# A decoder layer on one core: norm sums and rows placed apart, first MLP-down operands in freed buffers, residual loaded in gated halves

## The chip, the core and the metric

The kernel runs on one core of a Trainium2 chip. TensorE (PE) multiplies and has a queue of its own for weight loads (PEld); VectorE (DVE), ScalarE (ACT) and GpSimd (POOL) do the elementwise work; SyncE (SP) issues every DMA here, from one queue, in order. Each engine runs its instructions in the order in which the program holds them. The metric is the device time of one execution, in microseconds (us).

## The reference, cut to what matters

```python
u = rms_norm(h, norm_mix_g);  proj = u @ w_in          # attention and mLSTM mixers (left out)
h = h + mix @ w_out                                    # "out projection"
u = rms_norm(h, norm_mlp_g)
h = h + jnp.square(jax.nn.relu(u @ w_up)) @ w_down     # "MLP up", "MLP down"
gate = jax.nn.sigmoid(rms_norm(h, norm_ple_g) @ w_ple_gate)
h = h + gate * (p @ w_ple)                             # "gate"; p @ w_ple are the "pl products"
return rms_norm(h, final_norm_g)
# rms_norm(x, g) = x * rsqrt(mean(x*x) + eps) * g; x is 1024 tokens x 1024 features, w_up 1024 x 4096
```

## The kernel before

Activations lie transposed: 128 features on the partitions, 1024 tokens along a row, so `h` is 8 tiles of 128x1024 fp32. fp32 precision comes from splitting each operand into a high and a low part (`split`: a cast on ACT, L93, then a subtraction on DVE, L94) and multiplying three times (`mm3`: L102 high by high, L103 high by low, L104 low by high). A stage is therefore a chain: raw load by DMA, cast on ACT, subtraction on DVE, three matmuls of 128x512.

A norm has two parts on PE. The squares of all features are added into one tile `state`; its column sums are small matmuls with a vector of ones (`cs`, L125); DVE and POOL turn them into 1/sqrt per token (`ra`, `rb`; the power is L135, L963 or L1030); PE spreads these over all partitions by transposes (`bp`, L131) and ACT copies them out (`rB`). Where the norm stands ahead of a product its weight is folded into the operand and its row factor is multiplied into the product afterwards, so the products themselves need no `rB`.

From the out projection on the stages are, in order of time:

- the norm of MLP up: `rstd_rows` makes column sums and rows in one go;
- the pl products, 96 matmuls, copied out by ACT (L862);
- MLP up, 16 steps f. Each does seven products for a 2x2 block (a Strassen scheme, keys b11, t1, t2, b22, t3, b21, t4), 84 matmuls. POOL makes weight combinations (L753 to L755) and activation combinations (L790); ACT and DVE split both. After each step DVE multiplies by the norm rows (L886), ACT squares (L887), and the results and their four combinations are stored to the DRAM array `zd` in two DMAs (zz, L888; zt, L895);
- MLP down, again seven keys, each over 8 groups g of 24 matmuls. A group loads `y` from `zd` (L977) and weights (L911), and for four of the keys POOL subtracts weights (L925, L928, L932). At the end of a key DVE adds PSUM to `h` (L989). When a half row of `h` is complete (keys b22, t3, b21, t4), `ready` squares it, adds the square to `state` on POOL (L952) and splits it into `hp`;
- the gate: `rstd_half(1)` after t3 and `rstd_half(0)` after t4, products `pg`, and the final norm in three slices of tokens (512, 256, 256).

Each engine's order is made when the program is built: a list scheduler runs its own timeline over the written order and may move an instruction ahead of others. Buffers come from pools; a new tile that lies over an older one waits until the older one's last readers, DMAs included, are done.

Of the kernel before, what the change touches and what calls it, by code (L numbers as in the profile page):

```python
# [16 lines left out]
P = 128  # L17
# [28 lines left out]
def layer_kernel(ctx, tc, xT, wqk, wv, wvg, wmv, wmqk, wmo, wout, wup, wdown, wpg, wple, pT,  # L46
# [667 lines left out]
    with ExitStack() as tail:  # L714
        zp = tail.enter_context(tc.tile_pool(name="zp", bufs=2, reuse_waits="tile"))
        up_scope = ExitStack()
        wtc, zu, wta, wtb = [up_scope.enter_context(tc.tile_pool(name=n, bufs=2, reuse_waits="tile"))
                             for n in ("wtc", "zu", "wta", "wtb")]
        pmm = tail.enter_context(tc.tile_pool(name="pmm2", bufs=8, space=PSUM, reuse_waits="tile"))

        def ztile(name):
            return zu.tile([P, 2, T], F32, name=name, tag="z", bufs=4)

# [92 lines left out]

        def rstd_rows(state, times=None):
            cs = acc_tile("cs2")
            col_sum(cs, state)
            a = zp.tile([P, NB], F32, name="ra", tag="ra")  # L820
            b = zp.tile([P, NB], F32, name="rb", tag="rb")
            rstd_cols(b, cs[:, :NB], a)
            if times is not None:
                G.tensor_tensor(b, b, times, op=ALU.mult)
            dst = zp.tile([P, T], F32, name="rB", tag="rB", bufs=1)
            rows(dst, b)
            return dst

# [23 lines left out]
        wpl = [load_t(wple[k], "wpl") for k in range(2)]  # L852
        rB = rstd_rows(sqs, srec)

# [10 lines left out]


        OWN = (0, 14, 15)
        for f in range(FF // P // 2):
            z = ztile("zz")
# [16 lines left out]
            V.scalar_tensor_tensor(z, z, 0.0, rB.unsqueeze(1).to_broadcast([P, 2, T]), op0=ALU.max, op1=ALU.mult)  # L886
            S.activation(z, z, AF.Square)  # L887
            nc.sync.dma_start(zd[f, :, :4], z.rearrange("p a (c t) -> p (a c) t", t=CH))  # L888
            ts = ztile("zt").rearrange("p a (c t) -> p (a c) t", t=CH)
            c0, c1 = slice(0, CH), slice(CH, T)  # L890
            V.tensor_tensor(ts[:, 0], z[:, 0, c1], z[:, 0, c0], op=ALU.subtract)
            V.tensor_tensor(ts[:, 1], z[:, 1, c1], ts[:, 0], op=ALU.add)
            V.tensor_tensor(ts[:, 2], z[:, 0, c1], z[:, 1, c1], op=ALU.add)
            V.tensor_tensor(ts[:, 3], z[:, 1, c0], ts[:, 1], op=ALU.subtract)
            nc.sync.dma_start(zd[f, :, 4:], ts)  # L895
        up_scope.close()
# [3 lines left out]
        NG = FF // P // 4  # L900
        rawp, hlp = [tail.enter_context(tc.tile_pool(name=n, bufs=3, reuse_waits="tile")) for n in ("rawp", "hlp")]

        def stream(name, tag, bufs):
            return rawp.tile([P, T], F32, name=name, tag=tag, bufs=bufs)

        def parts(name, tag, src):
            return split([hlp.tile([P, T], F32R, name=name + i, tag=tag + i) for i in "hl"], src)

        def wraw(g, blk):
            r = stream("wd_r", "wr", 4)  # L910
            nc.sync.dma_start(r, wdown[g, blk])  # L911
            return r

        A11, A12, A21, A22 = range(4)
        SLOT = dict(b11=0, b21=2, b22=3, t1=4, t2=5, t3=6, t4=7)
        sp4 = [pair("s", F32) for _ in range(NG // 2)]
# [38 lines left out]
        def rstd_half(c):  # L955
            sl = slice(c * CH, (c + 1) * CH)
            n = NB // 2
            cs = acc_tile("cs2")
            col_sum(cs, state[:, sl], n=n)
            a = zp.tile([P, NB], F32, name="ra", tag="ra")  # L960
            b = zp.tile([P, NB], F32, name="rb", tag="rb")
            V.tensor_scalar(a[:, :n], cs[:, :n], 1.0 / D, EPS, op0=ALU.mult, op1=ALU.add)
            G.tensor_tensor(b[:, :n], a[:, :n], mhalf[:, :n], op=ALU.pow)  # L963
            bp = acc_tile("bp2")
            bcast_rows(bp, b, n)
            S.copy(rB[:, sl], bp)

        bank = {}
        for key in OPS:
# [5 lines left out]
            for g in range(NG):  # L975
                y = stream("y_r", "yr", 3)
                nc.sync.dma_start(y.rearrange("p (f t) -> p f t", t=CH),  # L977
                                  zd[2 * g:2 * g + 2, :, SLOT[key]].rearrange("f p t -> p f t"))
                yh, yl = parts("y", "y", y)
                wh, wl = parts("wd", "w", weights(key, g))  # L980
                for o in range(KT // 2):
# [17 lines left out]

        def embed(w, k, sl):  # L1000
            n = sl.stop - sl.start

            def ev(ps, c, sl):
                ga = small("ga")[:, :n]
                V.tensor_tensor(ga, ps, rB[:, sl], op=ALU.mult)
                S.activation(ga, ga, AF.Tanh, scale=0.5)
                V.scalar_tensor_tensor(ga, ga, 1.0, emb[k][:, sl], op0=ALU.add, op1=ALU.mult)
                V.scalar_tensor_tensor(h[k][:, sl], ga, 0.5, h[k][:, sl], op0=ALU.mult, op1=ALU.add)
            proj_chunk(pmm, w, hp, ev, "pg", sl)
            if k == 0:  # L1010
                if not fin:
                    fin.append(unit("fin", F32))
                S.activation(fin[0][:, sl], h[k][:, sl], AF.Square)
            else:
                sq = small("sq3")[:, :n]
                S.activation(sq, h[k][:, sl], AF.Square)
                V.tensor_tensor(fin[0][:, sl], fin[0][:, sl], sq, op=ALU.add)

        def final(i, sl):
            n = sl.stop - sl.start  # L1020
            nt = n // P
            cs = acc_tile("cs3")
            col_sum(cs, fin[0][:, sl], n=nt)
            a = zp.tile([P, nt], F32, name="ra3", tag="ra")
# [3 lines left out]
            else:  # L1028
                V.tensor_scalar(a, cs[:, :nt], 1.0 / D, EPS, op0=ALU.mult, op1=ALU.add)
            G.tensor_tensor(b, a, mhalf[:, :nt], op=ALU.pow)  # L1030
            bp = acc_tile("bp3")
            bcast_rows(bp, b, nt)
            rows = small("rows")[:, :n]
# [28 lines left out]

        for k in range(2):
            fetch(k)
        for c in (1, 0):
            for k in range(2):
                embed(ws[k], k, slice(c * CH, (c + 1) * CH))
        for k in range(2, KT - LATE):
            fetch(k)
            for c in range(NCH):  # L1070
                embed(ws[k], k, slice(c * CH, (c + 1) * CH))
# [89 lines left out]
```

## Time and profile before

| | us |
|---|---|
| median of 3 runs (lowest, highest) | 1453.23 (1449.82, 1454.43) |
| the profiled execution: time | 1451.09 |
| its span in the trace | 1449.3 |
| PE busy | 1350.0 (93%) |
| DVE busy | 987.5 (68%) |
| ACT busy | 621.9 (43%) |
| POOL busy | 415.3 (29%) |

The profile is of one execution. PE is busy for nearly the whole span, so what counts are the places where it stands idle and the places where its granted clock is below full. The two are seen in the table of PE's waits and in rows of its timeline: two matmuls of 128x512 in a row start 0.23 us apart at the full clock and 0.43 us apart at the lower one.

### The profile page before, as it was taken

To read this page: it belongs to the slowest core of one execution; us is meant where nothing else is said; L and a number is where in the kernel's file an instruction comes from. 1 tells how busy PE (TensorE), PEld (TensorE's weight loads), DVE (VectorE), ACT (ScalarE), POOL (GpSimd) and SP (SyncE) were. 2 spreads that over 40 slices of the span, in tenths; PEclk is the share of its full clock that TensorE was granted. 3 is DMA by queue.
4 is the path that set the end of the run, shared out by engine and by line. 5 is a ranking of instruction groups with operands and counts; after the bars stand their busy time and mean duration, and the time that the engine had idled before them with its cause. 6 is when DMAs were issued, how large, how long until landed. Compare 5 with 4: busy or idle time off the path is not lost.

```text
span 1449.3 us, 18272 instructions
## 1 busy us (share of the span) xinstructions
PE 1350.0 (93%) x6815; PEld 1135.3 (78%) x6815; DVE 987.5 (68%) x1462; ACT 621.9 (43%) x975; POOL 415.3 (29%) x261
## 2 busy tenths in 40 slices
PE   8999999999889998949999999995999999898996
PEld 6978988878788886737888888884888888686886
DVE  7788688599767874792476666674589856465455
ACT  6555545644454341344344443442333354343323
POOL 1522120231014220261244333440268423111002
PEclk9999999999999999978999999997999999899998
DMA  6111112123154367423344434447897647464113
GB/s 222 45 48 37 34 47 72 57 84 100 41 169 147 100 228 262 144 104 123 139 156 164 174 146 163 157 174 292 287 310 241 205 131 275 131 198 136 44 44 116
DMA packets 75689, 208.24 MB, mean 144 GB/s; under 512 B 7281, under 2 KB 17425, under 8 KB 70993
## 3 DMA queue, kind: packets, MB, share of 16 engines
q1 hardware_dynamic: 75600, 207.09, 41.5%
q8 instruction: 53, 0.87, 0.3%
q14 instruction: 36, 0.29, 0.1%
HBM read 146.74 MB, written 60.32 MB: 143 GB/s over the span
## 4 chain that ended last, share of the span: by engine, by line
PE 52%; DVE 9%; issue 8%; DMA 4%; POOL 2%; ACT 2%; SPq 0%; DVEq 0%; ACTq 0%; POOLq 0%
PE u L102 7%; PE u L103 7%; PE u L104 7%; PE d L102 7%; PE d L103 7%; PE d L104 7%; DMA in<-mixmd 1%; POOL state L952 1%; PE pl L103 1%; PE pl L102 1%; PE pl L104 1%; PE cs L125 1%; PE mo L102 1%; DMA wo_r<-wout 1%; PE mo L103 1%
## 5 line engine op out<-in xcount | busy, mean ns | idle before, releaser
L102 PE MATMUL d<-yh,wdh 128*128 128x512 f32 x448 | 176.5, 394 | 17.1 <-ACT wdh L93 17.1
L103 PE MATMUL u<-x,wuh 128*128 128x512 f32 x448 | 176.5, 394 | 0.0
L103 PE MATMUL d<-yl,wdh 128*128 128x512 f32 x448 | 176.3, 393 | 0.0
L104 PE MATMUL d<-yh,wdl 128*128 128x512 f32 x448 | 174.4, 391 | 0.0
L102 PE MATMUL u<-x,wuh 128*128 128x512 f32 x448 | 174.3, 395 | 0.0
L104 PE MATMUL u<-x,wul 128*128 128x512 f32 x448 | 171.2, 394 | 0.0
L94 DVE TENSOR_TENSOR wul<-wu_r,wuh 128x768 fp32r<-128x768 f32 (+1 forms) x64 | 71.6, 1119 | 90.0 <-ACT wuh L93 89.8
L102 PEld LDWEIGHTS d<-yh,wdh 128*128 128x128 f32 x448 | 85.2, 190 | 35.4 <-ACT wdh L93 17.6
L753 POOL TENSOR_TENSOR wu_r<-wu_r 128x512 f32<-128x512 f32 x32 | 49.6, 1549 | 211.4 <-DMA wu_r<-wup 176.0
L103 PEld LDWEIGHTS u<-x,wuh 128*128 128x128 f32 x448 | 84.5, 189 | 19.7
L102 PEld LDWEIGHTS u<-x,wuh 128*128 128x128 f32 x448 | 84.4, 188 | 19.7
L104 PEld LDWEIGHTS u<-x,wul 128*128 128x128 f32 x448 | 84.4, 188 | 19.7
L103 PEld LDWEIGHTS d<-yl,wdh 128*128 128x128 f32 x448 | 85.2, 190 | 18.4 <-DVE yl L94 0.6
L104 PEld LDWEIGHTS d<-yh,wdl 128*128 128x128 f32 x448 | 84.9, 189 | 17.7
L94 DVE TENSOR_TENSOR yl<-y_r,yh 128x1024 fp32r<-128x1024 f32 x56 | 92.3, 1648 | 8.0 <-ACT yh L93 7.9
L93 ACT CAST wuh<-wu_r 128x768 fp32r<-128x768 f32 (+1 forms) x64 | 60.4, 943 | 78.9 <-POOL wu_r L754 55.5
L94 DVE TENSOR_TENSOR wdl<-wd_r,wdh 128x1024 fp32r<-128x1024 f32 x32 | 44.8, 1399 | 70.5 <-ACT wdh L93 70.4
L412 ACT ACTIVATE pr<-pr,mn 128x128 f32<-128x128 f32 (+3 forms) x64 | 49.5, 774 | 56.1 <-PE av L415 30.4
L94 DVE TENSOR_TENSOR wdl<-s,wdh 128x1024 fp32r<-128x1024 f32 x24 | 54.1, 2255 | 24.5 <-ACT wdh L93 24.5
L93 ACT CAST wdh<-wd_r 128x1024 fp32r<-128x1024 f32 x32 | 33.6, 1051 | 85.2 <-PE d L103 60.0
L876 ACT COPY tmp<-u 128x512 f32<-128x512 f32 x48 | 28.0, 586 | 85.7 <-PE u L104 85.7
L93 ACT CAST yh<-y_r 128x1024 fp32r<-128x1024 f32 x56 | 58.7, 1048 | 12.3 <-DMA y_r<-zd 10.0
(368 smaller groups left out, 3633.4 us busy)
## 6 DMA issues: line engine op xcount, KB each, us to landing
wd_r<-wdown SPq DMA_DIRECT2D x72, 512.0 KB
y_r<-zd SPq DMA_DIRECT2D x56, 512.0 KB
wu_r<-wup SPq DMA_DIRECT2D x32, 512.0 KB
zd<-zz SPq DMA_DIRECT2D x16, 1024.0 KB
zd<-zt SPq DMA_DIRECT2D x16, 1024.0 KB
wm_r<-wmqk SPq DMA_DIRECT2D x8, 512.0 KB
wo_r<-wout SPq DMA_DIRECT2D x16, 256.0 KB
hs<-h SPq DMA_DIRECT2D x8, 512.0 KB
```

The source lines that it names most:

```text
L93: S.copy(hi, src)
L94: V.tensor_tensor(lo, src, hi.bitcast(F32), op=ALU.subtract)
L102: PE.matmul(ps, wh, xh, start=start, stop=False, skip_group_check=more)
L103: PE.matmul(ps, wh, xl, start=False, stop=False, skip_group_check=more)
L104: PE.matmul(ps, wl, xh, start=False, stop=stop, skip_group_check=more)
L125: PE.matmul(ps[:, off + j:off + j + 1], src[:, j * P:(j + 1) * P], ones, start=start, stop=stop and (start or j == n - 1))
L412: S.activation(pr[:, :nk], pr[:, :nk], AF.Exp, scale=-1.0, bias=mn[:, :1], accum_out=den)
L753: G.tensor_tensor(raw[:, 4:7:2], raw[:, 2:3].to_broadcast([P, 2, L]), raw[:, 1:4:2], op=ALU.subtract)
L876: S.copy(tmp[key], ps)
L952: G.tensor_tensor(state[:, sl], state[:, sl], sq, op=ALU.add)
```

## The change

It has five parts.

1. The norm of MLP up is cut in two. `rstd` (column sums and power) is called after the first step of MLP up, `rows` after the second, and the first step's multiplication, square and stores (`store(0)`) follow it. The pl products come straight after the out projection. The buffers of zz and zt become two pools, zu0 and zu1, taken by even and odd steps.
2. The first two groups' operands of MLP down are loaded into `unit` buffers that MLP up has freed by its last step, and split into `pair` buffers that it frees during that step. The split buffers of the other groups come from two pools: hl2, with two buffers, and hl1, with one, which every third group takes (g3 first) and which lies over zu1.
3. The residual `h`, loaded back in 8 DMAs of 512 KB during the last step of MLP up, is loaded in 16 halves. Ahead of each stands a one-element copy on POOL that reads the group's `yl`; the DMA waits for it.
4. `ready` adds the squares on DVE. `rstd_half(1)` is cut in two and written into key b21; the first three gate products of the second half of tokens, and two of the first half, stand around the other one.
5. At the end, the last tile's squares are not added on DVE but summed on PE by a second row of small matmuls, and a slice's column sums are placed after the first product of the next slice.

The core of the diff:

```diff
-        wtc, zu, wta, wtb = [...]
+        wtc, zu0, wta, wtb, zu1 = [...]
...
-        rB = rstd_rows(sqs, srec)
         for k2 in range(KT // 2):      # pl products
...
+            if f == FF // P // 2 - 2:
+                first = [(y_load(0, unit("y_r", F32), "b11"), w_load(0, unit("wd_r", F32), 0))]
             products([load_blocks(wup[f, i], "wu") for i in range(2)], X, ev, "u", own)
-            (multiply by rB, square, store, four combinations, store)
+            zs.append(z)
+            if f == 0:
+                rcols = rstd(sqs, NB, srec)
+                continue
+            if f == 1:
+                rB = zp.tile([P, T], F32, name="rB", tag="rB", bufs=1)
+                rows(rB, rcols)
+                store(0)
+            store(f)
+        first.append((y_load(1, unit("y_r", F32), "b11"), w_load(1, unit("wd_r", F32), 0)))
+        first = [[split(pair(n), r) for n, r in zip(("y", "wd"), raws)] for raws in first]
         up_scope.close()
-        rawp, hlp = [... bufs=3 each]
+        rawp, hl2, hl1 = [... for n, b in (("rawp", 3), ("hl2", 2), ("hl1", 1))]
         def parts(name, tag, src):
+            pool = hl1 if made[tag] % 3 == 1 else hl2
+            made[tag] += 1
...
         h = [unit("h", F32) for _ in range(KT)]
-        for k in range(KT):
-            nc.sync.dma_start(h[k], hs[k])
+        LOADS = {("b11", 1 + n): (2 * n, lo) for n in range(4)}
+        LOADS.update({("b11" if n < 3 else "t1", (5 + n) % NG): (2 * n + 1, hi) for n in range(4)})
+        LOADS.update({("t2", 1 + n): (2 * n, hi) for n in range(4)})
+        LOADS.update({("b21", 1 + n): (2 * n + 1, lo) for n in range(4)})
...
-                G.tensor_tensor(state[:, sl], state[:, sl], sq, op=ALU.add)
+                V.tensor_tensor(state[:, sl], state[:, sl], sq, op=ALU.add)
...
+                if (key, g) in LOADS:
+                    k, half_of = LOADS[key, g]
+                    G.tensor_copy(h[k][:1, half_of.start:half_of.start + 1], yl.bitcast(F32)[:1, :1])
+                    nc.sync.dma_start(h[k][:, half_of], hs[k, :, half_of])
...
-            if key == "t3":
-                rstd_half(1)
-        rstd_half(0)
+                if key == "b21" and g == 2:
+                    rcols = rstd(state[:, CH:], NB // 2)
+                if key == "b21" and g == 5:
+                    half_rows(1, rcols)
...
+        for k in range(AHEAD):                 # AHEAD = 3
+            embed(k, hi)
+        rcols = rstd(state[:, lo], NB // 2)
+        sums = [gate_sums(k, lo) for k in range(2)]
+        half_rows(0, rcols)
...
         for i, sl in enumerate(slices):
             for k in range(KT - LATE, KT):
-                embed(ws[k], k, sl)
+                embed(k, sl)
+                if i and k == KT - LATE:
+                    rcols = final_cols(i - 1, slices[i - 1])
             if i:
-                final(i - 1, slices[i - 1])
-        final(i, sl)
+                final(i - 1, slices[i - 1], rcols)
+        final(i, sl, final_cols(i, sl))
```

What stands where, on PE, between the out projection (o) and MLP up (u); `-` is before, `+` after:

```order
 L103 MATMUL o<-mixm,woh 128x512
 L104 MATMUL o<-mixm,wol 128x512
-L125 MATMUL cs_6617<-ones,state 128x1 x8
-L131 MATMUL bp_6632<-ident,rb 128x128 x4
-L131 MATMUL bp_6638<-ident,rb 128x128 x4
 L102 MATMUL pl<-pp,wplh 128x512
```

The eight column sums and the eight transposes no longer stand between the out projection and the pl products. The sums come inside the first step of MLP up:

```order
+L102 MATMUL u<-x,wuh 128x512
+L103 MATMUL u<-x,wuh 128x512
+L104 MATMUL u<-x,wul 128x512
+L102 MATMUL u<-x,wuh 128x512
+L125 MATMUL cs_6883<-ones,state 128x1 x8
 L103 MATMUL u<-x,wuh 128x512
 L104 MATMUL u<-x,wul 128x512
```

The transposes follow in the second step, again between products of MLP up.

On ACT, at the passage from MLP up to MLP down, before (L887 is the last step's square; 8963 to 8969 are g0, 8999 and 9005 g1, 9035 and 9041 g2, 9071 and 9077 g3):

```order
L887 ACTIVATE zz_8781<-zz_8781 128x2048
L93 CAST yh_8963<-y_r_8961 128x1024
L93 CAST wdh_8969<-wd_r_8967 128x1024
L93 CAST yh_8999<-y_r_8997 128x1024
L93 CAST wdh_9005<-wd_r_9003 128x1024
L93 CAST yh_9035<-y_r_9033 128x1024
L93 CAST wdh_9041<-wd_r_9039 128x1024
L93 CAST wdh_9077<-wd_r_9075 128x1024
L93 CAST yh_9071<-y_r_9069 128x1024
```

The groups' casts stand in the order g0, g1, g2, g3, all behind the last square. After the change (L884 is the last step's square; 8934 and 8937 are g1, 9032 and 9038 g2, 9108 and 9114 g4, 9146 and 9152 g5, 9070 and 9076 g3):

```order
L93 CAST y_8934<-y_r_8924 128x1024
L93 CAST wd_8937<-wd_r_8926 128x1024
L903 COPY tmp_8857<-u_8815 128x512
L909 COPY tmp_8884<-u_8815 128x512
L93 CAST yh_9032<-y_r_9030 128x1024
L93 CAST wdh_9038<-wd_r_9036 128x1024
L884 ACTIVATE zz_8788<-zz_8788 128x2048
L93 CAST yh_9108<-y_r_9106 128x1024
L93 CAST wdh_9114<-wd_r_9112 128x1024
L93 CAST wdh_9152<-wd_r_9150 128x1024
L93 CAST yh_9146<-y_r_9144 128x1024
L93 CAST yh_9070<-y_r_9068 128x1024
```

g1 and g2 now stand ahead of the last square, and g4 and g5 stand ahead of g3. g5's pair goes into the buffers of g2, and g3's into hl1.

## Rows read from the trace of the kernel before

**Rows 1.** PE's waits: us in total, times, longest.

```profile
PE d L102 <- ACT wdh L93: 17.1, 1, 17.1
PE cs L125 <- DVE state L809: 13.4, 1, 13.4
PE bp L131 <- POOL rb L824: 9.9, 1, 9.9
...
PE bp L131 <- POOL rb L1030: 4.5, 3, 1.8
...
PE o L102 <- ACT woh L93: 3.7, 1, 3.7
```

**Rows 2.** Windows: PE, PEld, DVE, ACT, POOL busy; clock; DMA share; GB/s.

```profile
657.10:680.00 22.90, 22.90 (x93) 18.47 (x92) 1.23 (x1) 9.87 (x17) 2.21 (x3) 0.91 0.42 160
...
700.00:993.00 293.00, 293.00 (x1263) 237.58 (x1262) 187.48 (x180) 116.89 (x133) 103.33 (x84) 1.00 0.44 167
...
1011.00:1056.00 45.00, 45.00 (x188) 37.04 (x189) 27.50 (x20) 18.23 (x18) 11.30 (x4) 0.94 0.84 299
...
1242.00:1330.00 88.00, 88.00 (x383) 72.66 (x383) 42.76 (x40) 35.57 (x41) 6.99 (x5) 0.98 0.52 166
...
1339.00:1413.00 74.00, 74.00 (x312) 59.89 (x310) 37.43 (x51) 21.23 (x31) 0.00 (x0) 0.97 0.13 43
```

**Rows 3.** Timeline of PE, out projection to pl products: start, duration, [idle before].

```profile
641.96 3.57 PE L125 MATMUL cs<-ones,state 128*128 128x1 f32 x16 [13.38 <-DVE state L809]
655.47 1.97 PE L131 MATMUL bp<-ident,rb 128*128 128x128 f32 x8 [9.93 <-POOL rb L824]
657.09 0.78 PE L102 MATMUL pl<-pp,wplh 128*128 128x512 f32 x1
```

**Rows 4.** Timeline of all engines, the same stretch.

```profile
639.67 0.33 SPq L752 DMA_DIRECT2D wu_r<-wup  x1
...
643.41 2.82 POOL L753 TENSOR_TENSOR wu_r<-wu_r 128x512 f32<-128x512 f32 x1 [5.46 <-DMA wu_r<-wup]
...
647.48 1.04 ACT L93 CAST x<-t 128x1024 fp32r<-128x1024 f32 x1 [9.80 <-POOL t L790]
```

**Rows 5.** Timeline of POOL, during the pl products.

```profile
677.64 1.29 POOL L753 TENSOR_TENSOR wu_r<-wu_r 128x512 f32<-128x512 f32 x1 [22.23 <-DMA wu_r<-wup]
```

**Rows 6.** Timeline of all engines, MLP up to MLP down.

```profile
1002.07 0.32 SPq L895 DMA_DIRECT2D zd<-zt  x1
1002.48 0.42 SPq L977 DMA_DIRECT2D y_r<-zd  x1
...
1008.67 1.04 ACT L93 CAST yh<-y_r 128x1024 fp32r<-128x1024 f32 x1 [9.28 <-DMA y_r<-zd]
...
1010.95 0.80 PE L102 MATMUL d<-yh,wdh 128*128 128x512 f32 x1 [17.12 <-ACT wdh L93]
```

**Rows 7.** Timeline of PE, end of key t3.

```profile
1237.60 1.87 PE L125 MATMUL cs<-ones,state 128*128 128x1 f32 x8 [5.95 <-POOL state L952]
1240.82 1.12 PE L131 MATMUL bp<-ident,rb 128*128 128x128 f32 x4 [1.35 <-POOL rb L963]
```

**Rows 8.** Timeline of PE, end of key t4.

```profile
1335.02 1.87 PE L125 MATMUL cs<-ones,state 128*128 128x1 f32 x8 [4.56 <-POOL state L952]
```

**Rows 9.** Timeline of PE, the final norm.

```profile
1426.13 0.41 PE L102 MATMUL pg<-hp,wpgh 128*128 128x256 f32 x1
...
1429.12 0.31 PE L104 MATMUL pg<-hp,wpgl 128*128 128x256 f32 x1
...
1439.16 0.82 PE L125 MATMUL cs<-ones,fin 128*128 128x1 f32 x4 [1.06 <-DVE fin L1017]
```

**Rows 10.** Timeline of POOL, keys t1 and t2.

```profile
1074.92 33.55 POOL L932 TENSOR_TENSOR s<-wd_r,s 128x1024 f32<-128x1024 f32 x10
```

**Rows 11.** Timeline of DVE, keys t1 and t2.

```profile
1092.72 3.42 DVE L94 TENSOR_TENSOR wdl<-s,wdh 128x1024 fp32r<-128x1024 f32 x1
...
1109.47 1.21 DVE L94 TENSOR_TENSOR yl<-y_r,yh 128x1024 fp32r<-128x1024 f32 x1
```

More of the change, by code (lines that the diff above doesn't have):

```diff
@@ L864, in layer_kernel, with y_load, w_load, store @@
             nc.sync.dma_start(ed[k2], e)
+        zs = []
+        SLOT = dict(b11=0, b21=2, b22=3, t1=4, t2=5, t3=6, t4=7)
+        def y_load(g, y, key):
+            nc.sync.dma_start(y.rearrange("p (f t) -> p f t", t=CH),
+                              zd[2 * g:2 * g + 2, :, SLOT[key]].rearrange("f p t -> p f t"))
+            return y
+        def w_load(g, r, blk):
+            nc.sync.dma_start(r, wdown[g, blk])
+            return r
+        def store(f):
+            z = zs[f]
+            V.scalar_tensor_tensor(z, z, 0.0, rB.unsqueeze(1).to_broadcast([P, 2, T]), op0=ALU.max, op1=ALU.mult)
+            S.activation(z, z, AF.Square)
+            nc.sync.dma_start(zd[f, :, :4], z.rearrange("p a (c t) -> p (a c) t", t=CH))
+            ts = ztile("zt", f % 2).rearrange("p a (c t) -> p (a c) t", t=CH)
+            c0, c1 = slice(0, CH), slice(CH, T)
+            V.tensor_tensor(ts[:, 0], z[:, 0, c1], z[:, 0, c0], op=ALU.subtract)
+            V.tensor_tensor(ts[:, 1], z[:, 1, c1], ts[:, 0], op=ALU.add)
+            V.tensor_tensor(ts[:, 2], z[:, 0, c1], z[:, 1, c1], op=ALU.add)
+            V.tensor_tensor(ts[:, 3], z[:, 1, c0], ts[:, 1], op=ALU.subtract)
+            nc.sync.dma_start(zd[f, :, 4:], ts)
         OWN = (0, 14, 15)
         for f in range(FF // P // 2):
-            z = ztile("zz")
+            z = ztile("zz", f % 2)
             tmp = {}
@@ L896, in layer_kernel @@
+            if f == 0:
[8 more added lines that the diff above has]
+        first = [[split(pair(n), r) for n, r in zip(("y", "wd"), raws)] for raws in first]
         up_scope.close()
         NG = FF // P // 4
[L901 removed]
+        rawp, hl2, hl1 = [tail.enter_context(tc.tile_pool(name=n, bufs=b, reuse_waits="tile"))
+                          for n, b in (("rawp", 3), ("hl2", 2), ("hl1", 1))]
@@ L975, in layer_kernel @@
             for g in range(NG):
[L976 to L980, printed above, removed]
+                if first:
+                    (yh, yl), (wh, wl) = first.pop(0)
+                else:
+                    yh, yl = parts("y", "y", y_load(g, stream("y_r", "yr", 3), key))
+                    wh, wl = parts("wd", "w", weights(key, g))
+                if (key, g) in LOADS:
+                    k, half_of = LOADS[key, g]
+                    G.tensor_copy(h[k][:1, half_of.start:half_of.start + 1], yl.bitcast(F32)[:1, :1])
+                    nc.sync.dma_start(h[k][:, half_of], hs[k, :, half_of])
                 for o in range(KT // 2):
@@ L1013, in embed, with final_cols @@
                 S.activation(fin[0][:, sl], h[k][:, sl], AF.Square)
-            else:
-                sq = small("sq3")[:, :n]
-                S.activation(sq, h[k][:, sl], AF.Square)
+                return
+            sq = small("sq3")[:, :n]
+            S.activation(sq, h[k][:, sl], AF.Square)
+            if k == KT - 1:
+                last[sl.start] = sq
+            else:
                 V.tensor_tensor(fin[0][:, sl], fin[0][:, sl], sq, op=ALU.add)
-        def final(i, sl):
-            n = sl.stop - sl.start
-            nt = n // P
+        def embed(k, sl):
+            gate(k, sl, gate_sums(k, sl))
+        def final_cols(i, sl):
+            nt = (sl.stop - sl.start) // P
             cs = acc_tile("cs3")
-            col_sum(cs, fin[0][:, sl], n=nt)
+            for j in range(nt):
+                for src in (fin[0][:, sl], last[sl.start]):
+                    PE.matmul(cs[:, j:j + 1], src[:, j * P:(j + 1) * P], ones, start=src is not last[sl.start],
+                              stop=src is last[sl.start])
             a = zp.tile([P, nt], F32, name="ra3", tag="ra")
@@ L1030, in final @@
             G.tensor_tensor(b, a, mhalf[:, :nt], op=ALU.pow)
+            return b
+        def final(i, sl, b):
+            n = sl.stop - sl.start
             bp = acc_tile("bp3")
-            bcast_rows(bp, b, nt)
+            bcast_rows(bp, b, n // P)
             rows = small("rows")[:, :n]
@@ L1061, in fetch @@
             ws[k] = split((unit("wpg"), unit("wpg")), r) if k == KT - 1 else parts("wpg", "w", r)
-        for k in range(2):
+        AHEAD = 3
+        for k in range(AHEAD):
             fetch(k)
[L1065 to L1068, printed above, removed]
+        for k in range(AHEAD):
+            embed(k, hi)
+        rcols = rstd(state[:, lo], NB // 2)
+        sums = [gate_sums(k, lo) for k in range(2)]
+        half_rows(0, rcols)
+        for k in range(AHEAD):
+            gate(k, lo, sums[k] if k < 2 else gate_sums(k, lo))
+        for k in range(AHEAD, KT - LATE):
             fetch(k)
             for c in range(NCH):
-                embed(ws[k], k, slice(c * CH, (c + 1) * CH))
+                embed(k, slice(c * CH, (c + 1) * CH))
         for k in range(KT - LATE, KT):
```

77 lines of the change are left out of this document (31 added, 46 removed).

## The prediction

> **What bounds the kernel now.** The table of busy times comes first: PE is busy for 93% of the span, so the kernel is bound by PE, and a change that adds no work to PE's rivals can only win PE's idle time and time at the lower clock. The table of PE's waits comes second, and shows where the idle time lies: 17.1 us at the passage from MLP up to MLP down, 13.4 and 9.9 at the norm ahead of MLP up [rows 1], 5.95 and 4.56 at the gate's norm [rows 7, 8], 4.5 in three pieces at the final norm [rows 1]. Together they are 55.4 us, and the change touches all of them. The windows come third: from 700 to 993 the clock is 1.00 and PE is never idle, so nothing is to be won or, as to the clock, lost in unbroken matmuls [rows 2]. The same row gives the pace: 293.0 us for 1263 matmuls, 0.232 us each. The clock has two levels, full and half (2.4 and 1.2 GHz). Where a window's mean is below 1.00, a part of it ran at half, and the time lost is the window times what the mean lacks to 1.00; the windows that begin behind PE's idle stretches have means of 0.91, 0.94, 0.98 and 0.97 [rows 2].
>
> **Out projection to MLP up (A).** Before, the last matmul of the out projection ends at 628.58 (641.96 less 13.38). PE waits 13.38 us for the sum of squares, spends 3.57 on column sums, waits 9.93 for the power, spends 1.62 on transposes until the first pl product at 657.09 [rows 3]: 28.5 us. The pl products then start at the lower clock: 0.09 of 22.9 us, 2.1 us lost [rows 2]. After the change pl follows the out projection at once: its weights are split by then, and the sums and transposes stand inside steps 0 and 1 of MLP up, where at full clock I take half of their time, 1.8 and 0.9 us. That is 28.5 + 2.1 - 2.7 = 27.9 us at best.
>
> What hid behind the wait and the pl products, though, is late next. The 96 pl products now end at 628.6 + 22.3 = 650.9, and step 0 needs split operands. In the trace of before its second weight block is asked for at 639.67, POOL combines it from 643.41 in 2.82 us, and ACT waits 9.80 us for POOL before it casts an activation combination at 647.48 [rows 4]. POOL's two later weight combinations and another activation combination follow at some 1.7 us each, and a cast and a subtraction of about 1 us each behind them, so the last operands for step 0 come at 655 to 656, with ACT's copies of the pl products in between. Of the 84 matmuls of step 0 (19.5 us) those that need them stand late; from the order I count a stall of about 2.7 us, and 1 us for the clock behind it. The bounds are none (27.9) and the 9.8 us that ACT waited there (18.1). I take 24.
>
> The same combination takes 2.82 us here beside busy DVE subtractions and 1.29 us when DVE is quiet [rows 4, 5]. The Trainium skill (SBUF — State Buffer, Who interferes with whom) gives a reason: a DVE instruction with two SBUF inputs and a GpSimd instruction that reads SBUF exclude each other for the whole instruction. By that rule the preparation of step 0 can't be squeezed, since the same instructions on both engines now stand in a shorter time; without it POOL would run at 1.29 and A would be 26 or 27. The trace agrees with the rule; A is taken from the rows above in any case.
>
> **MLP up to MLP down (B).** The last matmul of MLP up ends at 993.83. DVE, ACT and DVE again finish the last step, the zt store is issued at 1002.07, the first y load at 1002.48; it is cast at 1008.67 and PE starts at 1010.95 after 17.12 us [rows 6]. From 1011 to 1056 the mean clock is 0.94 [rows 2]: 0.06 of 45 us, 2.7 lost. The wait is worth 19.8 us. After the change g0 and g1 lie split in buffers of their own, g2 in hl2, and PE goes on without a break for three groups, 3 x 24 x 0.232 = 16.7 us.
>
> Then g3 is late. Its buffers hl1 lie over zu1, which the last step's zz and zt hold until their stores have landed, and on ACT its casts stand behind the two of g5, which wait until PE has done with g2's buffers. So at the earliest: 16.7, two casts of 1.04 us for g5, two for g3 [rows 6], PE goes on at 20.9, a stall of 4.2. The zt store can't land earlier than its issue, 8.2 us after the end of MLP up as before, and the 6.2 us that the y load took from issue to use [rows 6]: 14.4. Now it is queued on SP behind loads of the next groups; I place it at 12.6, landing at 19 to 22, and g3's first matmul at 21 to 24. So the stall is 4.2 to 7.4 us, and the clock costs 0 to 2.7 on top. B is 15.6 at best, 9.7 at worst if nothing else is late; I take 12.
>
> The idle times of 9.93, 17.12, 5.95 and 4.56 us [rows 3, 6, 7, 8] are each followed by a window of lower clock [rows 2]. The Trainium skill (TensorE: Matmul & The Clock Gate, HAM oscillation) says that a wait between bursts of matmuls puts PE back to half its clock, each time anew. By that rule this stall pays in full, 2.7 us where I take about 1.5, and the sum is 1.2 us less.
>
> **End of t3 (C) and of t4 (D).** At t3 PE waits 5.95 for POOL's additions of squares, sums for 1.87, waits 1.35 for the power and transposes until 1241.59 (0.77) [rows 7]: 9.94 us; the window behind it loses 0.02 of 88 us, 1.8 [rows 2]. At t4 it is 4.56 + 1.87 + 1.35 + 0.77 = 8.55 [rows 8, 7], and 0.03 of 74 us behind it, 2.2 [rows 2]. Sums and transposes come back at full clock among other products, at half of 1.87 and 1.12: 1.5 each time. The work that hides the chains is t4's groups of 5.6 us each for t3, and three gate products of 24 matmuls for t4. The squares are now added on DVE, three additions of 512 columns per key more, some 0.7 us each; splits run two groups ahead, so this is hidden. If that cover were gone, it would cost 2 us. C is 10 (8 to 11.5), D 9 (7 to 10.6).
>
> **Final norm (E).** Three waits for the power, 4.5 us [rows 1]; 1.06 for the last addition, and 3.0 us between 1426.13 and 1429.12 at which 256-column matmuls run at half pace [rows 9], 1.5 lost. The first two of the waits and the slow stretch can go, since another product now stands between sum and transposes; the last wait stays, and the last addition becomes a few small matmuls. Bounds 1 and 5.9; I take 3, because the last slice ends in a chain that no product covers.
>
> **The rest.** The 1 MB load for pl is issued before other transfers: PE waits 3.7 us for a cast of the out projection's weights [rows 1], behind casts that this load feeds; -2 to 1, I take 0.5. The sixteen gated half loads replace eight whole ones and carry the same bytes. They lie beside MLP down, where the DMA engines are busy for 0.84 of the time [rows 2]; 0 if SP stays ahead, -6 if a third of the gates hold a group back for an engine's instruction. I take 0.
>
> **Sum.** 24 + 12 + 10 + 9 + 3 + 0.5 = 58.5. The profiled execution took 1451.1 us, so 1392.6; it lies 2.1 below the median of the runs, and I predict 1395.
>
> **Rivals.** First, the passage to MLP down: the wait goes to g3 in full, because stores on the same queue land later still under 299 GB/s of loads [rows 2]. For it speaks that g3's buffers are the ones last freed; against it that 16.7 us of work stand ahead. B falls to 2: 1405.
>
> Second, MLP up: step 0 waits for its operands as long as ACT did, 9.8 us [rows 4], and step 1 too is late. A falls to 17: 1402. For it speaks that POOL and DVE are the slow ones there [rows 4, 5], against it that the first products need only what is ready early.
>
> Third, keys t1 and t2. There POOL runs ten subtractions in 33.55 us without a gap [rows 10], and a split on DVE takes 3.42 us where 1.21 is possible [rows 11]. Two splits are 6.84 us for a group that PE does in 5.57, so DVE falls behind by 1.27 a group, 6.4 us over the five groups of that stretch; before, the splits were far enough ahead that PE did not wait. Gates on POOL, a changed buffer count or later starts may use that reserve up: 6.4 us lost, 1401.
>
> Fourth, slower: the gates. SP issues in order, so a load that waits for a copy on POOL, which waits for a group's yl, holds the next groups' loads behind it. A POOL instruction ahead of the copy is 3.36 us [rows 10] and a load needs 6.2 [rows 6], 9.6 in all; two groups of reserve are 11.1 us. Were that reserve gone, each gate could cost 6.2, sixteen of them 99, and the time would be 1494. It decides the sign from 58.5 / 16 = 3.7 us per gate on.
>
> That the change does not do what it says is hardly open: the order shows sums and transposes between products. What it could still do is give each gain back at the next stage, since DVE at 68% and DMA bursts have room only on the average: about 1450.
>
> **How the numbers follow.** My forecast 0.56, the passage 0.17, step 0 0.12, t1 and t2 0.10, the gates 0.03, gains given back 0.02. The forecast's own range is 1386 to 1404; with the next three cases and the bounds of A and B (27.9 and 15.6 put it near 1387, together with E at 5.9 at 1384) the range is 1384 to 1412. Under 0.3% (4.4 us) a measurement of this kernel can't be told from no change. All cases but the last two are faster by far: faster 0.95, same 0.02, slower 0.03.
>
> **What would show it.** In the profile after: the row for L125 waiting for L809 and the one for L131 waiting for L824 are gone, pl starts at about 628.6, MLP up ends near 970 (A). PE's 17.1 us wait for wdh is gone and a wait of 4 to 7 us for a cast of MLP down stands some 16.7 us after the end of MLP up (B); if PE waits under 3 us or over 10 us there, that step is wrong. No wait above 2 us at cs and bp at the ends of t3 and t4 (C, D). Any wait of PE over 3 us in t1 or t2, on DVE or ACT, speaks for the third rival, and waits at regular distance of a group for y_r for the fourth. A time above 1412 would mean that a stage I hold to be covered is not.

## The result and the profile after

The changed kernel takes 1397.86 us (median of 4 runs, 1394.56 to 1398.74), the kernel before 1451.87 in the same series; the ratio is 0.962 (95% interval 0.960 to 0.965). The forecast was 1395. The profiled execution has a span of 1396.1 us, 53.2 shorter.

The busy times of the page: PE works as long as before and fills 97% of the span instead of 93%.

```profile
PE 1348.7 (97%) x6831; PEld 1130.6 (81%) x6831; DVE 982.8 (70%) x1473; ACT 620.3 (44%) x975; POOL 405.5 (29%) x263
```

PE's waits in the table of after (us in total, times, longest), which answer to [rows 1]:

```profile
PE d L102 <- ACT wdh L93: 3.7, 1, 3.7
...
PE o L102 <- ACT woh L93: 2.6, 1, 2.6
PE cs L1069 <- DVE fin L1059: 2.1, 1, 2.1
...
PE d L103 <- DVE yl L94: 1.4, 2, 0.9
PE u L102 <- ACT x L93: 1.4, 3, 0.9
...
PE bp L131 <- POOL rb L1077: 1.2, 1, 1.2
```

The rows of 13.4 and 9.9 us are gone, and the waits of the gate's norm with them; 17.1 us became 3.7, and small waits for casts and splits are new. Read in stages from PE's timeline, the 53.2 us lie here (each stage ends with the last matmul named):

| stage | before | after | gain | forecast |
|---|---|---|---|---|
| to the end of the out projection (F) | 628.6 | 627.5 | 1.1 | 0.5 |
| to the end of MLP up (A) | 365.3 | 345.4 | 19.8 | 24 |
| to the end of key t4 (B and C) | 336.6 | 314.9 | 21.7 | 22 |
| to the first 256-column gate product (D) | 83.2 | 73.6 | 9.6 | 9 |
| to the end (E) | 35.6 | 34.6 | 1.0 | 3 |

**A.** The timeline of PE after, at the place of [rows 3]:

```profile
627.12 0.39 PE L104 MATMUL o<-mixm,wol 128*128 128x512 f32 x1
627.35 0.40 PE L102 MATMUL pl<-pp,wplh 128*128 128x512 f32 x1
...
655.64 0.50 PE L102 MATMUL u<-x,wuh 128*128 128x512 f32 x1 [0.88 <-ACT x L93]
...
658.39 1.84 PE L125 MATMUL cs<-ones,state 128*128 128x1 f32 x16
...
663.46 0.80 PE L102 MATMUL u<-x,wuh 128*128 128x512 f32 x1 [0.24 <-ACT x L93]
```

pl follows the out projection 0.23 us later, and the column sums take 1.84 us in step 0, half of 3.57 as forecast. But step 0 waits five times for splits, and its matmuls behind the sums run at half clock. The windows show it (columns as in [rows 2]): from 651 to 700 the mean clock lacks 0.07 of 49 us, 3.4 us lost, and from 700 to 969 nothing.

```profile
651.00:700.00 49.00, 47.19 (x198) 36.52 (x197) 27.10 (x32) 24.59 (x37) 16.68 (x16) 0.93 0.26 97
700.00:969.00 269.00, 269.00 (x1154) 216.42 (x1153) 178.28 (x171) 112.81 (x127) 95.40 (x79) 1.00 0.47 173
969.00:1000.00 31.00, 27.25 (x108) 21.81 (x108) 15.48 (x16) 10.38 (x10) 3.46 (x4) 0.89 0.95 357
```

**B.** At the passage PE goes on without a break and stops 16.4 us later for 3.75 us, at g3, with half clock behind it (0.11 of 31 us, the wait included):

```profile
972.56 0.39 PE L104 MATMUL u<-x,wul 128*128 128x512 f32 x1
972.79 0.40 PE L102 MATMUL d<-y,wd 128*128 128x512 f32 x1
...
988.93 0.39 PE L104 MATMUL d<-yh,wdl 128*128 128x512 f32 x1
993.07 2.07 PE L102 MATMUL d<-yh,wdh 128*128 128x512 f32 x4 [3.75 <-ACT wdh L93]
```

ACT and SP at that moment:

```profile
984.32 0.32 SPq L892 DMA_DIRECT2D zd<-zt  x1
...
989.13 1.04 ACT L93 CAST wdh<-wd_r 128x1024 fp32r<-128x1024 f32 x1 [7.75 <-PE d L103]
990.08 1.99 ACT L93 CAST yh<-y_r 128x1024 fp32r<-128x1024 f32 x2
...
991.97 1.04 ACT L93 CAST wdh<-wd_r 128x1024 fp32r<-128x1024 f32 x1
```

ACT waits for PE's last use of g2's buffers (989.13), casts g5's weights and y, and only then g3's y and weights; 993.07 follows from that, by the steps of the forecast. The zt store, issued at 984.32, holds nobody.

**C and D.** Sums and rows stand in t4's first two groups, without a wait and at half their former time, and the gate products follow t4 directly [rows 7, 8]:

```profile
1244.57 0.95 PE L125 MATMUL cs<-ones,state 128*128 128x1 f32 x8
...
1252.76 0.60 PE L131 MATMUL bp<-ident,rb 128*128 128x128 f32 x4
```

```profile
1287.46 0.39 PE L104 MATMUL d<-yh,wdl 128*128 128x512 f32 x1
1287.68 0.40 PE L102 MATMUL pg<-hp,wpgh 128*128 128x512 f32 x1
```

The first 256-column product starts at 1361.49 after and at 1413.68 before:

```profile
1361.49 0.29 PE L102 MATMUL pg<-hp,wpgh 128*128 128x256 f32 x1
```

```profile
1413.68 0.29 PE L102 MATMUL pg<-hp,wpgh 128*128 128x256 f32 x1
```

### The profile page after: what moved, and what is told of

It reads as the page before. It is cut to its first block, busy times and chain, and to the rows that moved or that the text cites. A ratio compares the mean times of both kernels' runs of the same rounds, so it can differ in the third digit from the quotient of the medians.

```text
span 1396.1 us, 18322 instructions
## 1 busy us (share of the span) xinstructions
PE 1348.7 (97%) x6831; PEld 1130.6 (81%) x6831; DVE 982.8 (70%) x1473; ACT 620.3 (44%) x975; POOL 405.5 (29%) x263
## 5 line engine op out<-in xcount | busy, mean ns | idle before, releaser
L103 PE MATMUL u<-x,wuh 128*128 128x512 f32 x448 | 178.2, 398 | 0.4 <-DVE x L94 0.4
L102 PE MATMUL u<-x,wuh 128*128 128x512 f32 x448 | 176.4, 399 | 1.4 <-ACT x L93 1.4
L102 PE MATMUL d<-yh,wdh 128*128 128x512 f32 x432 | 168.9, 392 | 3.7 <-ACT wdh L93 3.7
L103 PE MATMUL d<-yl,wdh 128*128 128x512 f32 x432 | 169.0, 393 | 1.4 <-DVE yl L94 1.4
L104 PE MATMUL d<-yh,wdl 128*128 128x512 f32 x432 | 168.4, 391 | 0.0
L103 PEld LDWEIGHTS u<-x,wuh 128*128 128x128 f32 x448 | 84.7, 189 | 21.7 <-DVE x L94 1.3
L102 PEld LDWEIGHTS d<-yh,wdh 128*128 128x128 f32 x432 | 81.8, 190 | 21.3 <-ACT wdh L93 4.2
L103 PEld LDWEIGHTS d<-yl,wdh 128*128 128x128 f32 x432 | 81.8, 189 | 19.4 <-DVE yl L94 2.2
L104 PEld LDWEIGHTS d<-yh,wdl 128*128 128x128 f32 x432 | 81.5, 189 | 16.7
L94 DVE TENSOR_TENSOR yl<-y_r,yh 128x1024 fp32r<-128x1024 f32 x54 | 86.5, 1603 | 0.0
L94 DVE TENSOR_TENSOR wdl<-wd_r,wdh 128x1024 fp32r<-128x1024 f32 x30 | 38.2, 1273 | 65.3 <-ACT wdh L93 65.3
L93 ACT CAST wdh<-s 128x1024 fp32r<-128x1024 f32 x24 | 25.2, 1050 | 83.2 <-issue 48.1
```

Of the source, the lines that this page charges most:

```text
L93: S.copy(hi, src)
L94: V.tensor_tensor(lo, src, hi.bitcast(F32), op=ALU.subtract)
L102: PE.matmul(ps, wh, xh, start=start, stop=False, skip_group_check=more)
L103: PE.matmul(ps, wh, xl, start=False, stop=False, skip_group_check=more)
L104: PE.matmul(ps, wl, xh, start=False, stop=stop, skip_group_check=more)
```

## The experiments

Ratios have 95% intervals. The last two columns are read from PE's timeline: from the start of the last matmul of the out projection to that of MLP up, and from there to that of key t4.

| kernel | median us | ratio | up | down |
|---|---|---|---|---|
| before | 1451.9 | | 365.2 | 336.6 |
| changed | 1397.9 | 0.962 (0.960, 0.965) | 345.4 | 314.9 |
| norm_ahead | 1415.7 | 0.976 (0.974, 0.978) | 364.9 | 314.3 |
| no_first | 1399.3 | 0.965 (0.963, 0.966) | 344.5 | 318.0 |
| whole_h | 1398.0 | 0.963 (0.961, 0.965) | 344.3 | 315.0 |
| g4_last | 1393.1 | 0.960 (0.958, 0.961) | 343.9 | 312.1 |
| nf_one_z | 1411.7 | 0.971 (0.969, 0.973) | 344.6 | 326.9 |
| nf_whole_h | 1404.6 | 0.967 (0.964, 0.969) | 343.8 | 322.0 |
| three_rot | 1391.7 | 0.958 (0.955, 0.961) | 345.3 | 308.8 |
| sums_early | 1394.4 | 0.959 (0.957, 0.962) | 341.9 | 314.4 |
| best | 1390.4 | 0.958 (0.957, 0.960) | 342.6 | 308.8 |
| best_tail | 1389.1 | 0.957 (0.956, 0.959) | 342.6 | 309.4 |
| best_wpl | 1396.2 | 0.962 (0.960, 0.963) | 349.3 | 308.8 |
| pool_adds | 1396.2 | 0.962 (0.961, 0.964) | 345.1 | 314.8 |

Each ratio is to the kernel before as it ran in the same series. The out projection ended anywhere from 624.6 to 630.5 us in the profiles of the changed kernels, though no edit but best_wpl's touches what stands before it. The 1.1 us under F can't be told from that, and the medians are uncertain by 2 to 4 us, as the intervals say. So the two stage lengths decide.

**norm_ahead: the norm put back.**

```diff
         wpl = [load_t(wple[k], "wpl") for k in range(2)]
+        rcols = rstd(sqs, NB, srec); rB = ...; rows(rB, rcols)
...
-            if f == 0: ... (rstd)   if f == 1: ... (rows, store(0))
             store(f)
```

> The changed kernel (1397.9 us) with the norm of MLP up put back: column sums and rows both ahead of the pl products, every step stored at once. Theory: this part alone is worth the 19.8 us by which the stretch from the out projection to the end of MLP up became shorter, so about 1418 us (1415 to 1421), PE waits again 13 us for the state and 10 us for the power, and nothing behind MLP up changes. Rival: most of the gain there comes from the earlier load of the pl operands, and the time is 1406 or less.

"Up" grew by 19.4 us, "down" stayed, and both waits are back, nearly as in [rows 3]:

```profile
642.69 3.57 PE L125 MATMUL cs<-ones,state 128*128 128x1 f32 x16 [12.83 <-DVE state L812]
656.05 1.97 PE L131 MATMUL bp<-ident,rb 128*128 128x128 f32 x8 [9.79 <-POOL rb L828]
```

So A is this edit alone. The median is 17.9 above the changed kernel's, within the uncertainty just named.

**no_first, nf_one_z, nf_whole_h, whole_h: what shortened the passage.** no_first drops the early operands, and puts the split buffers of MLP down back into one pool of three:

```diff
-                first = [(y_load(0, ...), w_load(0, ...))]
-        first.append(...); first = [[split(pair(n), r) ...]]
+        first = []
-        rawp, hl2, hl1 = [...]
+        rawp, hlp = [... bufs=3 ...]
```

> The changed kernel without the early operands: no group of MLP down is loaded into freed buffers, and one pool of three split buffers as before. Theory: the wait of about 17 us for wdh comes back at the start of MLP down and the 3.75 us wait at g3 goes; 1397.9 + 11 to 13 = 1409 to 1411 us. Rival: the half loads of h, which no longer crowd the passage, are what shortened it; then the wait is 10 us or less and the time under 1404.

The theory fell: "down" grew by 3.1 us only. Without any early operand PE waits 7.49 us, not 17. The timeline of all engines shows why: the first y load is issued at 962.85, 8 us ahead of the end of MLP up, and the zt store of the last step only at 979.00; before, that load stood 0.41 us behind that store [rows 6].

```profile
962.85 0.40 SPq L872 DMA_DIRECT2D y_r<-zd  x1
...
978.25 2.08 PE L102 MATMUL d<-yh,wdh 128*128 128x512 f32 x4 [7.49 <-ACT wdh L93]
...
979.00 0.33 SPq L892 DMA_DIRECT2D zd<-zt  x1
```

Two edits could have done that: the two pools or, as the rival has it, the half loads of h. nf_one_z is no_first with one pool for zz and zt, as before; nf_whole_h is no_first with whole loads of h; whole_h is the changed kernel with whole loads of h:

```diff
-        wtc, zu0, wta, wtb, zu1 = [...]
+        wtc, zu, wta, wtb = [...]                 # nf_one_z
+        for k in range(KT):
+            nc.sync.dma_start(h[k], hs[k])        # nf_whole_h, whole_h
-                if (key, g) in LOADS: ...
```

> The changed kernel without the early operands (as no_first, 1399.3 us, PE waits 7.49 us at the passage) and with one pool of four zz and zt buffers, as in the kernel before, in place of the two pools zu0 and zu1; gated half loads of h stay. In the order on SP the first loads of MLP down now stand behind the last zt store again; in no_first they stood ahead of the last step's stores. Theory (the two pools free the raw buffers a step earlier, and that is what shortened the passage): the wait is 16 to 17.5 us and the time 1408 to 1411. Rival (the missing whole loads of h shortened it): the wait stays under 10 us, 1402 or less.

> As no_first, with the two pools, but h in eight whole loads where the kernel before has them. Theory (the pools): the wait stays at 7.5 to 10 us, 1399 to 1403. Rival (the loads of h): 14 to 17 us again, 1406 to 1410.

> The changed kernel with the residual loaded in 8 whole loads without gates, where the kernel before has them. Theory (the gates are worth nothing in themselves): the same bytes beside other work, within 1 us of 1397.9. Rival: the 4 MB, about 12 us of all DMA engines at 350 GB/s, stand ahead of the loads of g2 and g3 and of the last stores, PE waits longer at the passage, and the time is 1402 to 1407.

PE at the first product of MLP down, in nf_one_z and then in nf_whole_h:

```profile
989.78 0.80 PE L102 MATMUL d<-yh,wdh 128*128 128x512 f32 x1 [17.14 <-ACT wdh L93]
```

```profile
978.96 2.07 PE L102 MATMUL d<-yh,wdh 128*128 128x512 f32 x4 [7.50 <-ACT wdh L93]
...
986.27 0.80 PE L104 MATMUL d<-yh,wdl 128*128 128x512 f32 x1 [3.33 <-DVE wdl L94]
```

With one pool the whole wait is back, 17.14 us, though h is loaded in halves; "down" is 8.9 us longer than in no_first, and the median, 1411.7, is 0.7 above the theory's range. With two pools the wait stays at 7.50, and whole loads add 3.33 us at the next operand; "down" is 3.9 longer, and the time, 1404.6, lies between theory and rival. In whole_h, with the early operands in place, whole loads leave "down" as it was (315.0 against 314.9), but the waits have moved. PE waits 0.79 us at g2 and 5.57 at g3, where the changed kernel waits 3.75:

```profile
996.49 2.07 PE L102 MATMUL d<-yh,wdh 128*128 128x512 f32 x4 [5.57 <-ACT wdh L93]
```

In return the two waits in key t1, 1.4 us in the changed kernel, are gone, as they are in nf_whole_h (g4_last, with half loads, has none either). So the half loads shorten the passage, and the gain is not kept. Taken away in this order, the early operands are worth 3.1 us of "down" and the two pools 8.9 more. No run has the early operands with one pool; how much of the 8.9 us they would win alone is open.

**g4_last and three_rot: the wait at g3.**

```diff
-            pool = hl1 if made[tag] % 3 == 1 else hl2
+            pool = hl1 if made[tag] % 3 == 2 else hl2     # g4_last, three_rot
-        first.append((y_load(1, ...), w_load(1, ...)))
+        for g in (1, 2): first.append((y_load(g, ...), w_load(g, ...)))   # three_rot
```

> The changed kernel with the buffer hl1 taken by g4 instead of g3 (every third group from the third on). In the order on ACT g3 now stands right behind g2, but g4 stands behind g5 and g6. Theory (the wait at g3 comes from the order on ACT, where casts that wait for PE stand ahead): the wait moves to g4, about 4 us again, and the time stays at 1397 to 1399. Rival (the wait is for the last stores of MLP up to land): g4 is needed 5.6 us later than g3, the wait is gone or under 1 us, and the clock is not lost either: 1391 to 1394 us.

> The changed kernel with a third group's operands (g2) split ahead into pairs that MLP up frees, and hl1 taken by every third of the other groups from g5 on. On ACT g3 and g4 stand ahead, then g6, then g5; g6's casts wait until PE is done with g3, 22.3 us after the end of MLP up, so g5's are done at 26.5 and are needed at 27.9. Theory (casts that wait for PE stand ahead of the next group's, which makes the 3.75 us wait at g3, and at g4 in g4_last): no wait of PE over 1 us in the first key, the clock stays at full, 1391 to 1394 us. Rival (six raw loads during the last step come too late, or the last stores still hold hl1 then): a wait of 3 us or more stands elsewhere in the first key, 1396 to 1400.

In g4_last the same 3.75 us stand one group later:

```profile
994.61 1.61 PE L102 MATMUL d<-yh,wdh 128*128 128x512 f32 x4 [3.75 <-ACT wdh L93]
```

The wait moved as the theory says; that the time fell into the rival's range has other reasons. "Down" is 2.8 us shorter, with a clock of 0.97 instead of 0.94 from 950 to 1010 and without the 1.4 us of waits in t1; in the profiles "up" is 1.5 us shorter too, and the out projection ended 2.4 us earlier. three_rot takes away what makes g5's casts wait, and the passage runs without a wait at full clock:

```profile
950.00:1010.00 60.00, 60.00 (x264) 49.12 (x263) 41.08 (x41) 26.90 (x28) 8.30 (x10) 1.00 0.82 309
```

"Down" is 6.1 us shorter: 3.75 of wait, and 3.0 of clock, as its waits in t1 are 0.7 us longer. The order on ACT made the wait, not the last stores: g4_last moved the buffer that the stores hold to a group needed 5.6 us later, and the wait was as long as before.

**sums_early: the column sums among the pl products.**

```diff
             nc.sync.dma_start(ed[k2], e)
+            if k2 == 2:
+                rcols = rstd(sqs, NB, srec)
...
             if f == 0:
-                rcols = rstd(sqs, NB, srec)
```

> The changed kernel with the column sums of the norm of MLP up placed among the pl products, after 72 of them (some 644 us, the state is ready at 640.5), instead of in step 0. The pair of buffers that holds the state is taken by the operand b11 of the second half of the features, which waits for the sums. Theory (the sums standing late in step 0 hold up that operand, and this makes part of PE's eight short waits between 649 and 664 us and the lower clock from 661 to 668): the waits behind the sums go, the slow stretch goes, 2 to 4 us less from the out projection to MLP down, 1394 to 1396. Rival (POOL's and DVE's preparation alone is late): the waits stay, within 1 us of 1397.9.

Two waits are left of those in step 0:

```profile
661.67 0.50 PE L102 MATMUL u<-x,wuh 128*128 128x512 f32 x1 [1.41 <-ACT x L93]
662.93 0.61 PE L103 MATMUL u<-x,wuh 128*128 128x512 f32 x1 [0.76 <-DVE x L94]
```

"Up" is 341.9, and 342.6 in two more kernels with this edit, against 343.8 to 345.4 in eight without it: about 2 us, the theory's lower end. The slow stretch did not go (0.91 from 660 to 680), so that part of the theory fell. Of the eight waits that it names, PE's rows of the changed kernel show six. At g3 PE waits 5.65 us here, where the changed kernel waits 3.75, but only 0.52 in t1, and "down" is no longer than there.

**best, best_tail, best_wpl.** best is three_rot with sums_early.

> three_rot and sums_early in one kernel. They act at different places (three_rot: 6.1 us less in MLP down; sums_early: 3.5 us less from the out projection to MLP down), so their gains add: 1397.9 - 6.1 - 3.5 = 1388.3 us, 1386 to 1391, and faster than both kernels. Rival: the waits at step 0 or at the first key come back in another form (sums_early alone had 5.65 us at g3, where the changed kernel had 3.75): 1392 or more.

"Down" is three_rot's, 308.8; "up" is 342.6 beside 341.9, with a third wait in step 0 of 0.49 us. The 5.65 us at g3 did not come. Its five runs (1387.5 to 1393.0) lie below all four of the changed kernel; that it beats three_rot is not resolved.

best_tail gives DVE all output products of the first slice; best_wpl loads the pl weights through a zz buffer:

```diff
-        ON_V = ((0, 3, 6), range(KT), ...)
+        ON_V = (range(KT), range(KT), ...)                              # best_tail
-        wpl = [load_t(wple[k], "wpl") for k in range(2)]
+        wraws = ztile("wpl_r"); nc.sync.dma_start(wraws[:, k], wple[k]) # best_wpl
```

> best, with all eight output products of the first slice of the final norm on DVE and none on POOL. In the changed kernel three steps of the last slice's chain on DVE took 1.22, 1.41 and 1.45 us beside POOL's output products, and 0.42 us afterwards. Theory (POOL's products hold DVE up, and this is why the tail gave only 1.0 us): these steps take 0.42 us, and the time from the first 256-column product to the end, 34.6 us in every kernel so far, becomes 33.0 to 34.2. Rival (DVE is simply full: five more products of 0.7 us stand in its way): 35 to 37 us.

The changed kernel's tail, all engines: two steps of the chain take 1.22 and 1.41 us beside POOL's products (a third takes 1.45), and 0.42 later. POOL's row is the first, and the last two rows are the final norm's waits.

```profile
1374.90 5.23 POOL L1096 TENSOR_TENSOR out<-out,rows 128x512 f32<-128x512 f32 x4 [3.98 <-ACT rows L1085]
...
1377.76 1.22 DVE L1047 SCALAR_TENSOR_TENSOR ga<-ga,e 128x256 f32<-128x256 f32 x1
...
1379.00 1.41 DVE L1048 SCALAR_TENSOR_TENSOR h<-ga,h 128x256 f32<-128x256 f32 x1
...
1382.78 0.42 DVE L1048 SCALAR_TENSOR_TENSOR h<-ga,h 128x256 f32<-128x256 f32 x1
...
1384.26 0.35 PE L1069 MATMUL cs<-ones,fin 128*128 128x1 f32 x2 [2.05 <-DVE fin L1059]
...
1385.47 0.59 PE L1069 MATMUL cs<-ones,sq 128*128 128x1 f32 x2 [0.86 <-ACT sq L1055]
```

DVE in best_tail:

```profile
1363.58 5.35 DVE L1095 SCALAR_TENSOR_TENSOR out<-h,col,bp 128x512 f32<-128x512 f32 x8 [0.96 <-ACT rows L1087]
...
1369.76 0.43 DVE L1049 SCALAR_TENSOR_TENSOR ga<-ga,e 128x256 f32<-128x256 f32 x1 [0.42 <-ACT ga L1048]
1370.22 0.42 DVE L1050 SCALAR_TENSOR_TENSOR h<-ga,h 128x256 f32<-128x256 f32 x1
```

The steps take 0.42 to 0.43 us, so POOL's products did slow them, as the theory says. But the eight products take 5.35 us of DVE, where the three of best take 2.06, and the tail becomes 35.1 us instead of 34.6: the rival's range. What was won on the steps was lost on the products, and that the slow steps are why the tail gave so little is not shown.

> best, with the raw weights of the pl products loaded into a free zz buffer, not into the two raw buffers that the weights of MLP up use. The second weight block of step 0, asked for at 638 us when the pl weights were split, can then be loaded some 10 us earlier. Theory (step 0 waits for operands because POOL stands in order behind that block's load): the last waits in step 0, 1.41 and 0.76 us in sums_early, go, and 2 us or more are saved against best. Rival (POOL and DVE are full there, whatever the order): the waits stay and the time is best's within 1 us.

PE in best_wpl at the start of the pl products:

```profile
636.74 0.80 PE L102 MATMUL pl<-pp,wplh 128*128 128x512 f32 x1 [8.97 <-ACT wplh L93]
```

The weights of pl now come 9 us late. SP issues their loads at 627.63, right behind a store of h, where best issues the first at 615.15; what holds them there is not shown. The waits in step 0 are gone, but behind a 9 us delay this says nothing about POOL's order. The question stays open.

**pool_adds: squares added on POOL.**

> The changed kernel with the squares of the gate's norm added on POOL again, the sums and rows where the change has them. Theory (what counts at the ends of t3 and t4 is where the sums and rows stand, not which engine adds): no wait at cs or bp, and 1397.9 within 1.5 us. Rival (the slow additions on POOL delay the state and hold up DVE's splits): a wait at cs of 1 us or more, or 1400 to 1403.

```diff
-                V.tensor_tensor(state[:, sl], state[:, sl], sq, op=ALU.add)
+                G.tensor_tensor(state[:, sl], state[:, sl], sq, op=ALU.add)
```

No wait at cs or bp at the ends of t3 and t4, and both stages as in the changed kernel; the time is 0.2 us below the theory's range. So the engine that adds is not what C and D come from. That it is the place of the sums and rows rests on the rows before and after; no run puts them back.

## Why the prediction was right, and where it was off

- **The sum.** The stages gave 53.2 of the 58.5 us. Of the 5.3 that lack, 4.2 lie in A and 2.0 in E; the other stages came out 0.9 above their forecasts.
- **A, 24 forecast, 19.8 measured.** The mechanism held (norm_ahead). What was mis-sized is the lateness of step 0's operands, 2.7 us of waits with 1 us of clock behind them. The waits in step 0 and ahead of it add up to 2.2 us. The lower clock behind them cost 3.4 us by the window. And at each of the six waits the next matmul starts about 0.2 us later than its listed idle time says (654.36 to 655.64 is 1.28 us for 0.23 of pace and 0.88 idle), because a matmul is listed as 0.39 us long while the next one starts 0.23 after it. The rest of 27.9 less 19.8, 8.1 us in all, is 1.3 us that no row assigns. The clock is not a price of its own here. In pool_adds, with the same order on PE, it is 1.00 over the same stretch:

```profile
651.00:700.00 49.00, 45.60 (x201) 35.26 (x200) 27.81 (x32) 24.29 (x36) 16.57 (x16) 1.00 0.28 104
```

From 648 on PE waits nine times instead of six, 4.3 us as listed, and "up" is 345.1 for 345.4 (343.9 to 344.6 in no_first, nf_one_z and g4_last, whose clock is full there too). At full clock PE waits for the operands instead; it is they that come late.
- **B, 12 forecast, 11.5 measured** (21.7 less C). In the changed kernel the path is the predicted one: three groups without a break, then a wait at g3, 16.4 us after the end of MLP up and 3.75 long for 4.2 to 7.4. Of its two causes only the order on ACT is one. What the prediction had wrong is what the early operands are worth. I gave them the whole 17.1 us, "g0 and g1 lie split in buffers of their own"; without them, but with the two zz pools, PE waits 7.49 (no_first), and with one pool 17.14 (nf_one_z). The pools let the scheduler place the loads ahead of the last step's stores. The prediction priced them at nothing, and the sum doesn't notice, since both are in the change.
- **C, 10.** The 9.94 us and 1.8 of clock are gone; 0.95 and 0.60 came back: 10.2. **D, 9:** 9.6. pool_adds shows no share of the move of the additions to DVE in it.
- **E, 3 forecast, 1.0 measured.** The first two waits and the slow stretch went. From the first to the last 256-column product PE needs 20.2 us (1361.49 to 1381.71), 21.6 before (1413.68 to 1435.23). That is 1.3 us won where a wait of 1.5 and 1.5 of clock are gone: the sums now have two rows of small matmuls, and those of the first slice alone run for 1.6 us, where 0.95 stood before. Behind the last product 0.3 us are lost, though a wait of 1.8 is gone there [rows 1]. The wait for the last addition grew from 1.06 [rows 9] to 2.05, behind three DVE steps that ran beside POOL's products. The last sums, 0.82 us before [rows 9], take 2.65 (1384.26 to 1386.91), with a new wait of 0.86 for the last square in them. I had counted the added matmuls as "a few", and covered waits as won without asking what the chain now runs beside. PE's timeline before, the last product:

```profile
1435.23 0.28 PE L104 MATMUL pg<-hp,wpg 128*128 128x256 f32 x1
```

PE's timeline after, the first and last of the first slice's sums of the second row, and the last product:

```profile
1367.93 0.28 PE L1069 MATMUL cs<-ones,sq 128*128 128x1 f32 x2
...
1369.19 0.36 PE L1069 MATMUL cs<-ones,sq 128*128 128x1 f32 x2
...
1381.71 0.28 PE L104 MATMUL pg<-hp,wpg 128*128 128x256 f32 x1
```
- **The rules of the Trainium skill.** The Trainium skill (SBUF — State Buffer, Who interferes with whom) fits the tail: DVE steps with two SBUF inputs take 1.22 and 1.41 us while POOL's products run, and 0.42 without (best_tail). It also fits A's slow preparation, but no run isolates that. The other rule (the Trainium skill, TensorE: Matmul & The Clock Gate, HAM oscillation) fits the 3.75 us wait: half clock stands behind it, as behind the waits before, and cost 3.0 us by three_rot, nearer to the 2.7 worked out by the rule than to my 1.5.
- **Rivals.** The first two did not come: 3.75 us at g3, and no wait above 0.88 in step 0. The third came true in a small part: t1 has two waits for yl, 1.4 us of the 6.4 priced. PE's timeline after:

```profile
1067.47 0.50 PE L103 MATMUL d<-yl,wdh 128*128 128x512 f32 x1 [0.48 <-DVE yl L94]
...
1074.16 0.50 PE L103 MATMUL d<-yl,wdh 128*128 128x512 f32 x1 [0.92 <-DVE yl L94]
```

The fourth did not come: PE has no wait for y_r, and without the gates "down" is the same (whole_h). Whether the gates make the waits in t1 is open: both kernels with whole loads lack them, but so does g4_last.

## What to carry to other kernels

When two stages follow each other, ask which buffers of the second lie over buffers of the first, and when those come free: splitting one pool by turns let loads go out a step earlier and was worth 8.9 us of a passage, and loading the first operands into buffers of their own won 3.1 more on top of it. In an in-order queue an instruction that waits for the bottleneck engine must not stand ahead of one that the bottleneck waits for next; move the wait by giving its buffer to a later group. Price a wait with the clock behind it, and check what a covered stage now runs beside.

## What was not expected of the hardware

Behind four waits of under 1 us, with column sums among them, the granted clock fell to half from 661 to 668 us, but not in every execution: the mean from 660 to 680 is 0.83 in the changed kernel, and 1.00 in g4_last and pool_adds with the same order on PE and nearly the same four waits. And the stages up to the out projection moved the later ones by up to 5.9 us between the profiles of the changed kernels.
